# A decoder step on one core: the places of the depthwise convolution's VectorE steps

## The chip, the core and the metric

The kernel runs on one core of a Trainium2 chip. The metric is the device time of one execution in microseconds; less is better. A core has a matrix engine (PE, with its weight loads shown as PEld), a vector engine (DVE), a scalar engine (ACT), a general engine (POOL) and a sync engine (SP), which here does nothing but issue transfers from HBM. Each engine works through its own list of instructions in order, and waits for the others by semaphores.

## The reference

One layer of a decoder is computed for 512 prompt tokens and for 8 sequences of 4 new tokens each, 544 columns in all. Two branches read the same input projection: a convolution module and a stick-breaking attention. Cut to what matters here:

```
glu_a, glu_b, q, k, v, g_conv, g_att = split(x @ w_in)
u = glu_a * sigmoid(glu_b)                              # 512 channels
c = depthwise_conv(u, 31 taps) + conv_b                 # causal, per channel
conv_out = silu(layer_norm(c)) @ w_conv_proj
o = stick_breaking_attention(q, k, v)                   # samples: 4096 cached keys each
att_out = o @ w_att_proj
mixed = (sigmoid(g_conv) * conv_out + sigmoid(g_att) * att_out) @ w_out
x = layer_norm(alpha * x + mixed)
x = layer_norm(alpha * x + swiglu_ffn(x) + sigmoid(x @ w_ple_gate) * (p @ w_ple))
```

The cached keys and values of the samples lie in pages, 256 of keys and 256 of values, 256 KB each, which are found through a page table. They are 134 MB of the 222 MB that the kernel moves.

## The kernel before

Everything is held with the features on the 128 partitions and the tokens along the free axis. A dense product in near-full precision is made of three passes over a pair of parts, high and low, of both operands, so every weight tile is split by ACT (`wh`) and by DVE or POOL (`wl`) before PE uses it. Such a product writes a PSUM tile `g`; in the profile it reads `g<-xh,wh`, `g<-xl,wh`, `g<-xh,wl`. All products are recorded by `mm` (line 238), all transfers by `load` (line 228), and all DVE, ACT and POOL operations by one wrapper (line 146), so a reader goes by tile names rather than by lines.

The order of the instructions is written by a planner, the class `Weave`. It keeps one clock for PE (`wv.t`) and one for each other engine (`wv.dve`, `wv.act`, and `wv.dma` for transfers), and adds an assumed duration for each recorded operation. The work is a set of Python generators. The main one records the dense products; the side ones record the rest whenever the condition that they yielded last has come true on these clocks. So a condition decides where an instruction stands in its engine's list, and nothing of it is left at run time: on the chip an instruction waits for its operands and for its turn.

The generators that matter here:

- `main` makes the input projection in the order q, k, b, a, v for each of four groups of 128 channels, then the two sets of gates (tiles `ga`, `gc`), then the attention's projection (from the tiles `ohl`), then, after `yield done("conv")`, the convolution's projection (from `sh`, `sl`), then the output projection (tiles `m`), and from there the feed-forward part (`x1h`, `h`) and the embedding (`ph`).
- `prefetch` lets SP issue the pages, 32 groups of 8 key loads (`kv<-in_ck`) and 8 value loads (`kv<-in_cvv`) in turn. Every key load is preceded by the reading of a page number (line 657).
- `scores` and `decode` use them: group by group PE makes scores (`z<-kv`), ACT and DVE turn these into weights (`dz`, `dl`, `dp`), PE transposes them (`tp`) and multiplies with the values (`av<-kv`).
- `pa_pair` is the prompt's attention: scores into `z` and `tp`, weights `pa` with `pb` on ACT, DVE and POOL, sums into `o`. The values come by way of a transposition, which DVE copies out (`v<-tp`).
- `conv` is the depthwise convolution, all on DVE. For each of the four channel groups `i`, when its input `u` is there, it records 31 taps for the prompt's 512 columns (one `c<-u,cvt` and thirty `c<-u,cvt,c`), and two parts for the samples (`cs<-u`, `c<-cs`). Then follow the layer norm over all four groups (tiles `lnc`), the silu, and the split into `sh` and `sl`.

What paces `conv` before the change is one condition, tested after every second tap and before the sums of the samples' parts: `wv.dve < wv.t + CAHEAD`, that is, DVE's planned backlog is under 2.5 us (`CAHEAD`, line 1698). The generator has priority 3, behind those of the pages (0, 1) and of the attention (2).

Of the kernel before, what the change touches and what calls it, by code (L numbers as in the profile page):

```python
# [63 lines left out]
class Weave:  # L64
# [7 lines left out]
    def on(self, *aps):  # L72
        return At(max(self.ready.get(a.name, 0.0) for a in aps))
# [102 lines left out]
def step_kernel(ctx: ExitStack, tc: tile.TileContext, xT, pT, ck, cvv, state, pt, W, cv, cc, yT, kT, vT, cvo):  # L176
    nc = tc.nc
    wv = Weave()
# [10 lines left out]
    def done(f):  # L189
        return lambda: f in flag  # L190

    def spare(n):

        return lambda: cur["t"] <= 4 - n

    def drop():
        cur["t"] -= 1

    def slot(name, shape=(128, 2, NT), dt=F32):
        return big.tile(list(shape), dt, tag="s", bufs=NSLOT, name=name)  # L200

    def tmp(name):
        cur["t"] += 1
        return big.tile([128, NT], F32, tag="t", bufs=4, name=name)
# [42 lines left out]
    def calm():  # L247
        return max(wv.act, wv.dve) < wv.t + CALM

# [25 lines left out]
    def split(hi, lo, src, *then, eng=None):  # L275
        n = size(src)
        near = src.space != PSUM
        if near and end("dve", (n / 2 + 66) / 960, src) + VBIAS < end("act", (n + 112) / 1200, src):
            V.tensor_copy(out=hi, in_=src)
        else:  # L280
            S.activation(out=hi, in_=src, func=AF.Copy)

        def low():
            (tt if near and eng is None else V.tensor_tensor)(out=lo, in0=src, in1=hi.bitcast(F32), op=ALU.subtract)
            flag.update(then)
        if not then:
            low()
        else:
            wv.when(on(hi), low)

    def sigmoid(out, in_, t, t2, then, more=None):

        r = tmp("r")[:, :t.shape[1]]
        S.activation(out=t2, in_=in_, func=AF.Abs)
        r2 = halves(r) if len(in_.shape) == 3 else r
        n = size(in_)
        if end("dve", (n + 66) / 960, in_) + VBIAS < end("act", (n + 112) / 1200, in_):
            V.tensor_scalar(out=r2, in0=in_, scalar1=-1.0, scalar2=0.0, op0=ALU.mult, op1=ALU.max)
        else:
            S.activation(out=r2, in_=in_, func=AF.Relu, scale=-1.0)  # L300
        S.activation(out=t, in_=t, func=AF.Exp, scale=-1.0)
        S.activation(out=t, in_=t, func=AF.Ln, bias=1.0)

        def last():
            S.activation(out=out, in_=t, func=AF.Exp, scale=-1.0)
            flag.add(then)
            if more is not None:
                wv.when(on(out), more)

        def mid():  # L310
            tt(out=t, in0=r, in1=t, op=ALU.add)
            drop()
            wv.when(on(t), last)
        wv.when(on(t), mid)
# [551 lines left out]
    silu = []  # L866

    def conv():
        for g in range(2):
            c2 = slot("c")  # L870
            for e in range(2):
                i = 2 * g + e
                yield done(("u", i))
                u = us.pop(i)
                c = c2[:, e]
                a_ = c[:, 0:512]
                b_ = c[:, 512:544].rearrange("p (s q) -> p s q", q=4)
                us_ = u[:, 542:814].rearrange("p (s c) -> p s c", c=34)
                for k in range(KW):
                    w = cvt[:, CW + i * KW + k:CW + i * KW + k + 1]  # L880
                    a = u[:, k:k + 512]
                    if k == 0:
                        bb = cvt[:, CB + i:CB + i + 1]
                        V.tensor_scalar(out=a_, in0=a, scalar1=w, scalar2=bb, op0=ALU.mult, op1=ALU.add)
                    else:
                        V.scalar_tensor_tensor(out=a_, in0=a, scalar=w, in1=a_, op0=ALU.mult, op1=ALU.add)
                    if k % 2:
                        yield lambda: wv.dve < wv.t + CAHEAD
                for s in range(0, 8, 4):
                    yield spare(1)  # L890
                    t = tmp("cs")[:, :16 * KW].rearrange("p (s q k) -> p s q k", q=4, k=KW)
                    for q in range(4):
                        V.tensor_tensor(out=t[:, :, q], in0=us_[:, s:s + 4, q:q + KW],
                                        in1=cvt[:, CW + i * KW:CW + (i + 1) * KW].unsqueeze(1)
                                        .to_broadcast([128, 4, KW]), op=ALU.mult)
                    yield lambda: wv.dve < wv.t + CAHEAD
                    V.tensor_reduce(out=b_[:, s:s + 4], in_=t, op=ALU.add, axis=mybir.AxisListType.X)
                    del t
                    drop()
                V.tensor_scalar(out=b_, in0=b_, scalar1=cvt[:, CB + i:CB + i + 1], scalar2=None, op0=ALU.add)  # L900
                yield lambda: wv.dve < wv.t + CAHEAD
                del u, us_, a
                if i == 1:
                    tot = big.tile([128, NT], F32, tag="tot", bufs=1, name="tot")
                    V.tensor_tensor(out=tot, in0=c2[:, 0], in1=c2[:, 1], op=ALU.add)
                elif i > 1:
                    V.tensor_tensor(out=tot, in0=tot, in1=c, op=ALU.add)
            cp.append(c2)
        f = [slot("lnc") for i in range(3)]

        def each(g):
            x = cp[g]
            for e in range(2):
                i = 2 * g + e
                V.tensor_scalar(out=x[:, e], in0=x[:, e], scalar1=cvt[:, CG + i:CG + i + 1],
                                scalar2=cvt[:, CBB + i:CBB + i + 1], op0=ALU.mult, op1=ALU.add)
        yield from norm(cp, 2.0, NT, "o", f, tot, each, pace=calm)
        for g in range(2):
            yield on(cp[g])
            for e in range(2):  # L920
                t = f[g][:, e]
                yield calm
                yield spare(1)
                sigmoid(t, cp[g][:, e], t, t, ("silu", g, e))
                yield
        for g in range(2):
            x, t = cp[g], f[g]
            for e in range(2):
                yield done(("silu", g, e))
            yield on(t)  # L930
            yield calm
            V.tensor_tensor(out=x, in0=x, in1=t, op=ALU.mult)
            h, lo = slot("sh", dt=F32R), slot("sl", dt=F32R)
            yield on(x)
            split(h, lo, x, ("sl", g))
            silu.extend((h[:, e], lo[:, e]) for e in range(2))
        yield done(("sl", 0))
        yield done(("sl", 1))
        cp.clear()
        flag.add("conv")  # L940
# [146 lines left out]
    def residual():  # L1087
        x_hl.clear()
        for g in range(4):
            yield lambda: wv.dve < wv.t + CAHEAD  # L1090
            h, lo = (t.bitcast(F32) for t in x_tiles[g])
            r = slot("rr")
            V.tensor_tensor(out=r, in0=h, in1=lo, op=ALU.add)
            x_tiles[g] = h = lo = None
            yield lambda: wv.dve < wv.t + CAHEAD
            V.tensor_scalar(out=r, in0=r, scalar1=ALPHA, scalar2=None, op0=ALU.mult)
# [7 lines left out]
    def main():  # L1104
# [61 lines left out]
        vs = v2 = None  # L1166
        wv.add(prompt_attention(), 2)
        wv.add(conv(), 3)
        for w, m in ORDER:
            o = []  # L1170
# [525 lines left out]
GBIAS = 0.3  # L1696
DMA_AHEAD = 5.0
CAHEAD = 2.5
CALM = 1.5
WAHEAD = 5  # L1700
PSTEP = 1.0
# [106 lines left out]
```

## Time and profile before

| | |
|---|---|
| Median of 3 runs | 993.13 us (991.53 to 996.7) |
| The profiled execution's own time | 992.45 us |
| Its span | 990.6 us |
| Mean granted PE clock in it | 0.986 |
| PE busy | 950.3 us (96%) |
| DVE busy | 781.3 us (79%) |
| ACT busy | 539.2 us (54%) |
| POOL busy | 163.2 us (16%) |
| Moved by DMA | 222 MB, 224 GB/s over the span |
| The chain of waits that ended last | PE 74%, DVE 10%, DMA 9%, SP's queue 3% |

The span reaches from the first to the last instruction; the execution's own time is 1.85 us longer. A busy PE is not PE at its peak, since matmuls are pipelined and their ends are modelled. The kernel has two halves. Up to about 555 us pages stream in and everything shares the engines; from about 580 us on PE works through the feed-forward part almost without a pause. The convolution's taps lie between 43 and 266 us, its norm and silu between 267 and 373 us.

### The profile page before, as it was taken

How to read it: one execution, taken by the hardware profiler on the slowest of the kernel's cores; microseconds unless marked ns; L12 is line 12 of the kernel's file. 1: busy time of each engine (PE TensorE's matmuls, PEld its weight loads, DVE VectorE, ACT ScalarE, POOL GpSimd, SP SyncE). 2: the span in 40 equal slices, each digit the busy share in tenths (PEclk: the TensorE clock that was granted, in tenths of full speed). 3: DMA queues.
4: the chain of work that ended last, by engine and by line, in shares of the span. 5: the costliest groups of instructions: out<-in, count | busy, mean ns of one | idle time of the engine just before them, and what ended most of it. 6: DMA issues, size and time to landing. Idle time of an engine off the chain costs nothing.

```text
span 990.6 us, 22509 instructions
## 1 busy us (share of the span) xinstructions
PE 950.3 (96%) x8026; PEld 831.2 (84%) x8026; DVE 781.3 (79%) x1288; ACT 539.2 (54%) x1042; POOL 163.2 (16%) x147
## 2 busy tenths in 40 slices
PE   9989999999899999999999889999999999999995
PEld 7866566667677887788878789999999999999994
DVE  3798798999964666466698687999999999943366
ACT  4634766575786785244467564544554555622224
POOL 1230313223211102033343110000000000220020
PEclk9999899999999999999999899999999999999998
DMA  9948989999989999999999635223223221322302
GB/s 356 339 160 298 336 301 330 313 324 328 311 281 339 311 346 330 342 367 351 325 335 352 250 108 193 86 88 126 86 91 123 86 95 56 100 93 87 128 1 90
DMA packets 101393, 222.00 MB, mean 224 GB/s; under 512 B 11169, under 2 KB 14498, under 8 KB 101282
## 3 DMA queue, kind: packets, MB, share of 16 engines
q1 hardware_dynamic: 99410, 217.46, 62.5%
q10 hardware_dynamic: 1872, 3.11, 0.8%
q8 instruction: 63, 1.03, 0.4%
q14 instruction: 48, 0.39, 0.1%
HBM read 215.45 MB, written 5.07 MB: 223 GB/s over the span
## 4 chain that ended last, share of the span: by engine, by line
PE 74%; DVE 10%; DMA 9%; SPq 3%; issue 2%; ACT 2%; POOL 0%; ACTq 0%; DVEq 0%; POOLq 0%
PE g L238 44%; PE z L238 10%; PE av L238 9%; PE o L238 5%; PE tp L238 5%; DVE c L146 3%; DMA kv<-in_cvv 2%; SPq L228 2%; DMA kv<-in_ck 2%; DVE pb L146 2%; DMA wr<-in_W 2%; PE tp L243 1%; DMA xr<-in_xT 1%; SPq L657 1%; DMA wa<-in_W 1%
## 5 line engine op out<-in xcount | busy, mean ns | idle before, releaser
L146 ACT ACTIVATE wh<-wr 128x512 fp32r<-128x512 f32 x236 | 146.9, 628 | 201.1 <-PE g L238 99.8
L146 DVE TENSOR_TENSOR wl<-wr,wh 128x512 fp32r<-128x512 f32 x196 | 135.1, 694 | 52.1 <-ACT wh L146 50.8
L146 POOL TENSOR_TENSOR wl<-wr,wh 128x512 fp32r<-128x512 f32 x44 | 70.2, 1598 | 493.0 <-DVE pw L146 259.8
L238 PE MATMUL g<-xh,wh 128*128 128x272 f32 (+1 forms) x512 | 127.6, 320 | 0.3 <-ACT wh L146 0.3
L238 PE MATMUL g<-h,wh 128*128 128x272 f32 x704 | 122.2, 290 | 0.0
L238 PE MATMUL g<-xl,wh 128*128 128x272 f32 (+1 forms) x512 | 119.3, 304 | 0.8 <-DVE xl L146 0.8
L238 PE MATMUL g<-xh,wl 128*128 128x272 f32 (+1 forms) x512 | 118.8, 303 | 0.2 <-POOL wl L146 0.2
L146 DVE SCALAR_TENSOR_TENSOR c<-u,cvt,c 128x512 f32<-128x512 f32 x120 | 111.6, 930 | 3.3
L238 PEld LDWEIGHTS g<-h,wh 128*128 128x128 f32 x704 | 103.2, 189 | 0.3
L238 PEld LDWEIGHTS g<-xh,wh 128*128 128x128 f32 x512 | 82.9, 191 | 22.2 <-issue 17.5
L238 PEld LDWEIGHTS g<-xl,wh 128*128 128x128 f32 x512 | 83.7, 191 | 3.6 <-DVE xl L146 1.5
L238 PEld LDWEIGHTS g<-xh,wl 128*128 128x128 f32 x512 | 83.1, 191 | 4.0 <-POOL wl L146 0.9
L238 PE MATMUL g<-h,wl 128*128 128x272 f32 x352 | 80.1, 289 | 0.0
L146 ACT ACTIVATE wh<-wq 128x512 fp32r<-128x512 f32 x87 | 54.5, 628 | 40.5 <-PE g L238 29.5
L238 PE MATMUL z<-kv,qblk 128*32 128x256 f32 x1024 | 64.6, 381 | 1.1 <-DMA kv<-in_ck 1.1
L238 PE MATMUL g<-x1h,wh 128*128 128x272 f32 (+2 forms) x216 | 64.0, 296 | 0.0
L238 PE MATMUL av<-kv,dp 128*32 128x512 f32 x512 | 63.8, 612 | 0.0
L146 DVE TENSOR_TENSOR wl<-wq,wh 128x512 fp32r<-128x512 f32 x75 | 54.6, 733 | 11.4 <-ACT wh L146 11.0
L238 PE MATMUL g<-x1l,wh 128*128 128x272 f32 (+2 forms) x216 | 62.6, 290 | 0.0
L238 PE MATMUL g<-x1h,wl 128*128 128x272 f32 (+2 forms) x216 | 62.6, 290 | 0.0
L146 ACT ACTIVATE pa<-pa 128x384 f32<-128x384 f32 (+1 forms) x96 | 52.5, 555 | 17.2 <-DVE pa L146 15.6
L238 PEld LDWEIGHTS g<-h,wl 128*128 128x128 f32 x352 | 58.0, 188 | 0.0
(315 smaller groups left out, 2352.8 us busy)
## 6 DMA issues: line engine op xcount, KB each, us to landing
kv<-in_ck SPq DMA_DIRECT2D x256, 256.0 KB, 4.4
kv<-in_cvv SPq DMA_DIRECT2D x256, 256.0 KB, 5.4
wr<-in_W SPq DMA_DIRECT2D x98, 512.0 KB, 4.2
wq<-in_W SPq DMA_DIRECT2D x37, 512.0 KB, 5.1
wa<-in_W SPq DMA_DIRECT2D x12, 512.0 KB, 10.2
xr<-in_xT SPq DMA_DIRECT2D x8, 272.0 KB, 5.6
out_yT<-pw SPq DMA_DIRECT2D x6, 272.0 KB, 2.3
out_kT<-qk ACTq DMA_DIRECT2D x4, 272.0 KB, 6.1
```

What stands on the lines that cost most here:

```text
L146: fn(**kw)
L228: eng.dma_start(out=out, in_=in_)
L238: T.matmul(out, lhsT=lhsT, rhs=rhs, start=start, stop=stop)
L243: T.transpose(out, in_, ident)
L657: reg[col] = nc.sync.value_load(ptt[0:1, col:col + 1], min_val=0, max_val=POOL - 1)
```

## The change

The pace of `conv` is set otherwise. A counter runs through the steps of the convolution: 31 taps and 2 sample parts for each channel group, 132 steps in all. After step n the generator now yields until the planner's PE clock has reached `CONV_T0 + n * CONV_DT`, that is 20 + 1.9 n us, and DVE's planned backlog is under `CAHEAD` as before. The condition now stands after every tap, where it stood after every second one. The last step may so be recorded from 270.8 us of the planner's clock on. No operation is added, removed or resized.

```
     def conv():
+        step = [0]
+
+        def even():
+
+            step[0] += 1
+            t = CONV_T0 + step[0] * CONV_DT
+            return lambda: t <= wv.t and wv.dve < wv.t + CAHEAD
         for g in range(2):
...
                         V.scalar_tensor_tensor(out=a_, in0=a, scalar=w, in1=a_, op0=ALU.mult, op1=ALU.add)
-                    if k % 2:
-                        yield lambda: wv.dve < wv.t + CAHEAD
+                    yield even()
                 for s in range(0, 8, 4):
...
-                    yield lambda: wv.dve < wv.t + CAHEAD
+                    yield even()
                     V.tensor_reduce(out=b_[:, s:s + 4], in_=t, op=ALU.add, axis=mybir.AxisListType.X)
...
 CAHEAD = 2.5
+CONV_T0 = 20.0
+CONV_DT = 1.9
```

Since the planner decides by its clocks, other generators' instructions move too. Three places are shown, as the engines' lists have them before and now.

DVE, the start of the second channel group (`u` is its input, `c` its sums, `dp`, `dl`, `dz` the weights of a group of pages, `pb` and `pa` the prompt's attention). Before:

```order
L146 TENSOR_SCALAR c<-u,cvt 128x512
L146 SCALAR_TENSOR_TENSOR c<-u,cvt,c 128x512 x9
L146 TENSOR_TENSOR wl<-wq,wh 128x512
L146 TENSOR_SCALAR dp<-dz 128x256
L146 SCALAR_TENSOR_TENSOR dl<-dl,cnew,dp 128x256
L146 TENSOR_TENSOR dz<-dz,dl 128x256
```

Now:

```order
L146 TENSOR_SCALAR c<-u,cvt 128x512
L146 SCALAR_TENSOR_TENSOR c<-u,cvt,c 128x512 x2
L146 CAST wh<-wq 128x512
L146 SCALAR_TENSOR_TENSOR c<-u,cvt,c 128x512
L146 TENSOR_SCALAR pb<-pa 128x512
L146 SCALAR_TENSOR_TENSOR pb<-pb,pa 128x512
L146 TENSOR_TENSOR pa<-pa,pb 128x512
L146 TENSOR_SCALAR dp<-dz 128x256
```

A run of ten taps ahead of the next weights has become one of three and a single one.

PE, the first scores of a group of pages (`z<-kv`; `tp<-cct,anew` is a transposition, the `g` products belong to the input projection). Before:

```order
L243 MATMUL tp<-cct,anew 128x128
L238 MATMUL g<-xh,wh 128x512
L238 MATMUL g<-xl,wh 128x512
L238 MATMUL g<-xh,wl 128x512
L238 MATMUL g<-xh,wh 128x272 x2
L238 MATMUL g<-xl,wh 128x272 x2
L238 MATMUL g<-xh,wl 128x272 x2
L238 MATMUL z<-kv,qblk 32x256 x16
```

Now:

```order
L243 MATMUL tp<-cct,anew 128x128
L238 MATMUL g<-xh,wh 128x512
L238 MATMUL g<-xl,wh 128x512
L238 MATMUL g<-xh,wl 128x512
L238 MATMUL g<-xh,wh 128x512
L238 MATMUL g<-xl,wh 128x512
L238 MATMUL g<-xh,wl 128x512
L238 MATMUL z<-kv,qblk 32x256 x16
```

Six products of 272 columns that stood ahead of the first scores now stand behind them; the three of 512 columns stood ahead of the transposition before.

PE, the last scores of a group of pages (the `ph` products are the embedding's, the `x1h` ones the feed-forward part's). Before:

```order
L238 MATMUL g<-ph,wh 128x272 x2
L238 MATMUL g<-pl,wh 128x272 x2
L238 MATMUL g<-ph,wl 128x272 x2
L238 MATMUL z<-kv,qblk 32x256 x16
L238 MATMUL o<-ln,on_m 128x256
```

Now:

```order
L238 MATMUL g<-x1h,wh 128x256
L238 MATMUL g<-x1l,wh 128x256
L238 MATMUL g<-x1h,wl 128x256
L238 MATMUL z<-kv,qblk 32x256 x16
L238 MATMUL g<-x1h,wh 128x256
L238 MATMUL g<-x1l,wh 128x256
L238 MATMUL g<-x1h,wl 128x256
```

The last scores have moved ahead, past products that now follow them: counted from the program's start, 2292 products `g` stood ahead of the last scores, and 2247 do now.

## The prediction

> **What bounds the kernel now.** I read the table by stretches first: it tells which stage of the 990.6 us could move at all. Its columns are the stretch, then busy time of each engine, the granted PE clock, the DMA share and GB/s.
>
> ```profile
> core 0: us, PE busy (x) PEld busy (x) DVE busy (x) ACT busy (x) POOL busy (x), PEclk, DMA share, GB/s
> 50.00:275.00 225.00, 206.94 (x1752) 152.82 (x1751) 205.76 (x329) 135.90 (x282) 57.70 (x55) 0.97 0.87 301
> 275.00:400.00 125.00, 124.15 (x1093) 98.36 (x1091) 81.32 (x122) 92.85 (x179) 19.79 (x18) 1.00 0.93 323
> 400.00:545.00 145.00, 143.94 (x1256) 116.14 (x1259) 101.32 (x164) 74.52 (x155) 44.55 (x38) 1.00 0.97 345
> 600.00:990.60 390.60, 378.72 (x2989) 377.50 (x2988) 321.43 (x528) 175.18 (x304) 21.92 (x11) 0.99 0.27 95
> ```
>
> DVE is 91% busy from 50 to 275 us and 65% in the next stretch; the DMA engines are at 87%, 93% and 97%. After 600 us only PE matters. The same stretches for the tile `c` alone show what the convolution takes of DVE:
>
> ```profile
> 50.00:275.00 225.00, 117.19 (x133) 0.97 0.87 301
> 275.00:400.00 125.00, 14.32 (x12) 1.00 0.93 323
> ```
>
> It is 57% of DVE's work in the stretch where DVE is full. Next the waits of PE between 45 and 275 us (who waited for what: us, times, longest):
>
> ```profile
> PE tp L243 <- DVE v L146: 7.8, 4, 4.4
> PE tp L243 <- ACT pa L146: 6.3, 3, 2.2
> PE z L238 <- ACT dz L146: 2.2, 1, 2.2
> PE tp L238 <- ACT dp L146: 0.8, 1, 0.8
> PE o L238 <- DVE tot L146: 0.7, 1, 0.7
> ```
>
> These 17.8 us are pauses of PE behind DVE, directly or by way of ACT. If PE alone set the end, they would be the prize. But the pages also have to arrive. SP's own queue shows what that takes:
>
> ```profile
> 332.15 8.67 SPq L228 DMA_DIRECT2D kv<-in_ck  x8
> ...
> 342.61 0.36 SPq L228 DMA_DIRECT2D wr<-in_W  x1
> 343.16 3.07 SPq L228 DMA_DIRECT2D kv<-in_cvv  x5
> 347.08 0.34 SPq L228 DMA_DIRECT2D kv<-in_ck  x1
> ```
>
> One group of pages keeps SP issuing from 332.15 to 347.08, without a pause worth the name: 8.67 us for eight key loads, 3.07 for five value loads. So the stream of pages has a pace of its own, some 15 us a group, that no DVE work enters unless SP itself waits. And PE is tied to it. Two rows show the scores of a group halted until its keys land; between 290 and 425 us such halts are all that is left of PE's waits for pages:
>
> ```profile
> 299.46 1.89 PE L238 MATMUL z<-kv,qblk 128*32 128x256 f32 x26 [0.26 <-DMA kv<-in_ck]
> 389.52 1.89 PE L238 MATMUL z<-kv,qblk 128*32 128x256 f32 x26 [0.59 <-DMA kv<-in_ck]
> PE z L238 <- DMA kv<-in_ck: 0.8, 2, 0.6
> ```
>
> I conclude that before the feed-forward half two things end together, PE's list and the stream. A pause of PE that is removed before 299 us is mostly given back as a halt there, unless the stream comes earlier too. The first half's end is so a matter of SP's waits.
>
> **The change, part by part.** Nothing is added: the same DVE instructions stand elsewhere. The convolution's taps last 0.75 us as a median, and the mean is higher because some take over 1.5. By the order, tap 31 stands behind 306 products `g` (294 before), tap 62 behind 570 (450), tap 93 behind 780 (672) and tap 124 behind 1065 (900). Before, the last tap stood behind 14 groups of scores; tap 106 stands there now. So 18 of 124 taps leave the full stretch. At the mean of the group, 117.19 us over 133, they are 16 us of 205.76: DVE falls from 91% to 84% there, and rises from 65% to 78% after it. The relief is modest.
>
> The first term is the longest wait of SP, between 62 and 100 us, with PE's and DVE's lists around it:
>
> ```profile
> SPq L228 <- PE z L238: 13.6, 2, 13.4
> 43.78 4.81 DVE L146 SCALAR_TENSOR_TENSOR c<-u,cvt,c 128x512 f32<-128x512 f32 x5
> 49.10 3.53 DVE L146 SCALAR_TENSOR_TENSOR c<-u,cvt,c 128x512 f32<-128x512 f32 x2
> 57.36 0.68 DVE L146 COPY v<-tp 128x512 f32<-128x512 f32 x1
> 64.22 0.41 PE L238 MATMUL g<-xh,wh 128*128 128x272 f32 x2
> 65.06 1.93 PE L238 MATMUL z<-kv,qblk 128*32 128x256 f32 x32
> ```
>
> SP stands still for 13.4 us because all page buffers are full and the first scores have not read them; these stand in PE's list behind a transposition whose bank DVE's `v` copy frees at 58 us, and that copy stands behind eight taps. The order now has eight taps there again: the grid of 20 + 1.9 n has already run past the first steps when `u` comes, so it holds nothing back. That wait therefore stays but for the six products of 272 columns that left their place ahead of the scores: from 64.22 to 65.06, **0.8 us**.
>
> The second term is SP's other waits between 80 and 350 us:
>
> ```profile
> SPq L228 <- DVE wl L146: 4.5, 2, 2.4
> SPq L228 <- DMA out_vT<-vt: 3.5, 1, 3.5
> SPq L228 <- DMA out_kT<-qk: 1.9, 1, 1.9
> SPq L228 <- POOL wl L146: 1.8, 2, 1.2
> ```
>
> The splits on DVE and POOL are 6.3 us, and a less crowded DVE can make them end earlier; the two at DVE lie in the stretch that now gets the last taps, though. Bounds: nothing, or, with the stores that ACT issues late, all 11.7. I take a third of the splits, **2.1 us**, nearer to nothing because of where they lie.
>
> The third term is bytes and issues: ahead of the last page 59 weight loads stand in SP's order where 60 stood. By the rows of SP's queue one costs 0.55 us of its time (342.61 to 343.16); by the 345 GB/s of the stretch its 512 KB cost 1.5. I take **1.0 us**. The stream so ends 3.9 us earlier.
>
> Against this, the price on the other side. The rows around the last scores:
>
> ```profile
> 523.75 1.48 SPq L228 DMA_DIRECT2D kv<-in_ck  x2
> 532.70 1.93 PE L238 MATMUL z<-kv,qblk 128*32 128x256 f32 x32
> 536.59 0.28 PE L238 MATMUL g<-x1h,wh 128*128 128x256 f32 x1
> 536.71 0.28 PE L238 MATMUL g<-x1l,wh 128*128 128x256 f32 x1
> kv<-in_ck SPq DMA_DIRECT2D x256, 256.0 KB, 4.4
> ```
>
> The last key load is issued at 524.9 (the second of the two from 523.75) and, at the median of 4.4 us, lands at 529.3; the scores start at 532.70, 3.4 us after it. Now 45 products fewer stand ahead of them, at 0.12 us each (536.59 to 536.71) **5.4 us**, which PE has to do afterwards. PE could come to the last scores at 532.7 - 5.4 = 527.3, less what it gains in pauses. The stream allows 529.3 - 3.9 + 0.3 (a halt as at 299 us) = 525.7. Half of the 13.4 us of pauses behind the first `v` copy would bring PE there, so I take the stream. Behind the last scores stood 990.6 - 532.7 = 457.9 us; now there are 5.4 more. The sum is 525.7 + 457.9 + 5.4 = 989.0 us of span, 1.6 less than before. With the 1.85 us around the span and the 0.7 us by which the median lies above the profiled execution this is **991.5 us**.
>
> The Trainium skill speaks against the second and third term: its page "DMA: Bandwidth & Descriptors", section "Issuing engines are not separate DMA queues", says that the time which the sequencer takes to initiate a transfer is usually small beside the transfer. By it SP's waits would be hidden under the queue and the weight load would cost its bytes; the sum would be 0.8 + 1.5 = 2.3 us of stream and a median of 993.1. The rows of SP's queue, solid for 15 us a group, disagree, so I keep the terms.
>
> What the moved work is hidden behind: the 16 us of taps that go past 275 us lie in a stretch with 43 us of idle DVE (125 less 81.32). What is late next is the silu. Its cover is read from these rows:
>
> ```profile
> L238 PE MATMUL g<-sh,wh x64: 282/288/394, 419.4 to 449.3; 128*128 128x272 f32 x64
> L146 DVE TENSOR_TENSOR sl<-c,sh x2: 1278/1832/2387, 367.9 to 370.9; 128x1088 fp32r<-128x1088 f32 x2
> 386.81 0.63 PE L238 MATMUL g<-ohl,wh 128*128 128x512 f32 x2
> ...
> 387.51 0.63 PE L238 MATMUL g<-ohl,wh 128*128 128x512 f32 x2
> ```
>
> Before, the split ended at 373.3 and its reader started at 419.4, 46 us later. In the order now 44 products from `ohl` (three from 386.81 to 387.51, 0.23 each, 10 us) and one group's scores and values (under 4) stand between: 14 us.
>
> **The rivals.** *Faster, because both bounds give way.* The pauses vanish and every SP wait listed above goes with them: the stream gains 0.8 + 11.7 + 1.0 = 13.5, the span is 990.6 - 3.4 + 0.3 + 5.4 - 13.5 = 979.4, the median 982; with two thirds of the waits, 986. For it speak the pauses, and the clock that falls behind one of them, where PE's share of a stretch of 10 us, the granted clock and the DMA share read:
>
> ```profile
> 100.00:110.00 10.00, 9.17 (x48) 0.70 1.00 344
> ```
>
> Against it: only 7 points of DVE's load go, and two of the four SP terms are stores or lie late. In a sentence of its own: "Perfetto Trace Analysis", section "Optimization Strategy", in the Trainium skill would have it so, since it tells to relieve the engines that PE idles for.
>
> *Slower, because the silu comes too late.* The convolution's projection waits in PE's list, and everything behind it, the pages' scores too. It decides once the norm and silu run over 14 us later than their place in the order. They took from 267 to 373 us; now the chain has to fit between about 315 and 407, while DVE is at 78% and not 65%. A lateness of 22 us would cost 8: 999. Against it: DVE has not lagged by more than the 4.4 us of the longest `v` pause.
>
> *Nothing moves in time.* The grid is on the planner's clock; if the chip is always behind it, the backlog condition alone decides and the list differs by chance. Then only the six products and the unit come off the stream, 1.8 us, and PE halts for it: 529.3 - 1.8 + 0.3 + 457.9 + 5.4 = 991.1 of span, a median of 993.6.
>
> **How the numbers follow.** Forecast 0.55, its own range 986 to 995: 986 with 5.5 us more of SP's waits gone, 995 with nothing of the stream gained. Faster rival 0.27, silu 0.12, nothing moves 0.06. A measurement of this kernel tells about 0.5% from no change, 5 us. Faster by more: nine tenths of the rival and 0.15 of the forecast, 0.33. Slower by more: most of the silu's 0.12 and a little of the rest, 0.13. Within: 0.54. For 8 in 10 the range reaches to the full price of the faster rival, 982, and on the other side nearly to the silu's and to the 998.5 of a stream that gains nothing while the last scores still start 3.4 us behind their keys: 998.
>
> **What would show it.** Right: SP's wait for `z` stays near 13 us; PE's waits for `v` and `pa` shrink, yet PE halts more for `in_ck` between 290 and 540 us; the last key load is issued some 4 us earlier; DVE at 84% up to 275 us. Wrong: the 13.4 us wait gone (then the faster rival), a wait of PE for `sl` at `g<-sh` (the silu), or a stream whose last key load comes later than at 524.9.

## The result and the profile after

The changed kernel takes **1007.73 us** (median of 4 runs, 1004.59 to 1013.15) against 992.8 for the kernel before beside it: 1.0154 times as long, 95% interval 1.0124 to 1.0183. It is slower, by 1.5%. The profiled execution is the slowest of the four, 1013.15 us with a span of 1011.4, so its rows show some 5 us more than the median has.

The table by stretches of the changed kernel, with the columns of the one shown of before:

```profile
core 0: us, PE busy (x) PEld busy (x) DVE busy (x) ACT busy (x) POOL busy (x), PEclk, DMA share, GB/s
50.00:275.00 225.00, 208.63 (x1765) 149.88 (x1764) 194.90 (x318) 136.11 (x282) 55.45 (x54) 0.98 0.88 296
275.00:400.00 125.00, 120.38 (x1061) 96.69 (x1059) 80.93 (x126) 86.73 (x170) 17.22 (x13) 1.00 0.94 324
545.00:600.00 55.00, 41.83 (x454) 37.05 (x453) 43.91 (x82) 26.81 (x62) 17.09 (x16) 0.94 0.48 184
```

DVE has fallen to 87% of the first stretch (91% before). But PE now idles 4.6 us between 275 and 400 us (0.9 before), and 13 of the 55 us from 545 on. To compare at equal work I cut both executions at two points of PE's list: the first product of the attention's projection (`g<-ohl`, 22 groups of scores ahead of it in both) and the first of the feed-forward's pairs (`z<-x1h`). Before, and then after:

```profile
45.00:385.20 340.20, 321.85 (x2777) 246.22 (x2776) 278.36 (x442) 225.25 (x454) 72.82 (x64) 0.98 0.89 308
385.20:609.30 224.10, 216.62 (x1925) 180.77 (x1924) 164.52 (x281) 119.62 (x248) 59.11 (x54) 0.98 0.84 300
609.30:990.60 381.30, 369.42 (x2920) 368.20 (x2918) 314.19 (x516) 170.55 (x295) 21.92 (x11) 0.99 0.26 90
```

```profile
45.00:387.90 342.90, 324.06 (x2777) 244.94 (x2777) 270.01 (x441) 220.68 (x448) 68.78 (x62) 0.99 0.90 306
387.90:630.00 242.10, 221.47 (x1922) 182.59 (x1921) 174.21 (x287) 120.95 (x247) 60.22 (x58) 0.97 0.78 277
630.00:1011.40 381.40, 369.44 (x2920) 368.23 (x2918) 314.64 (x516) 170.44 (x295) 21.72 (x11) 0.99 0.26 89
```

The last stretch is the same to 0.1 us. The first, where the change was made, is 2.7 us longer, but that is no more than the spread between executions: a_hold and a_pace below, whose lists are the same up to that point by their traces, reach it at 384.8 and 385.5 us. The middle one is **18.0 us longer**: PE idles 20.6 us of it instead of 7.5, and the same work takes it 4.9 us more, at a granted clock of 0.97 instead of 0.98. So the loss lies behind the convolution's taps, in a stretch where the change moved nothing on purpose.

Of PE's waits for DVE between 385 and 640 us, those that grow most, before:

```profile
PE g L238 <- DVE sg L146: 2.5, 1, 2.5
PE g L238 <- DVE pw L146: 0.7, 1, 0.7
```

and after:

```profile
PE g L238 <- DVE sg L146: 7.6, 3, 4.1
PE g L238 <- DVE ga L146: 4.8, 1, 4.8
PE g L238 <- DVE pw L146: 2.1, 1, 2.1
```

Two places carry 9.9 of the 13.1 us by which the pauses grow. The first is the drain of a gate's product into `ga`, whose bank PE needs for the attention's projection. DVE and PE around it:

```profile
397.30 1.69 DVE L146 TENSOR_SCALAR rr<-rr 128x1088 f32<-128x1088 f32 x1
398.91 1.29 DVE L146 TENSOR_TENSOR rr<-xh,xl 128x1088 f32<-128x1088 f32 x1
400.23 1.67 DVE L146 TENSOR_SCALAR rr<-rr 128x1088 f32<-128x1088 f32 x1
401.82 0.68 DVE L146 TENSOR_TENSOR ga<-g,ga 128x512 f32<-128x512 f32 x1
402.56 1.22 PE L238 MATMUL g<-ohl,wh 128*128 128x512 f32 x2 [4.80 <-DVE ga L146]
```

The residual's operations (`rr`, recorded by `residual`) stand ahead of the drain and PE halts 4.8 us. Before, the convolution's norm was long over there; now its tail (`lnc`, up to 394 us) and the residual share DVE just ahead of `ga`. Before, the first drain began 9.0 us after the first `g<-ohl` (385.18):

```profile
394.18 0.68 DVE L146 TENSOR_TENSOR ga<-g,ga 128x512 f32<-128x512 f32 x1
```

Now it begins 13.9 us after it (387.93). Three of the four scalings of the residual take 1.67 to 1.77 us each, where all four took at most 0.73 before: some 3 us of the delay. The second place is the embedding (`g<-ph`), whose bank waits for the feed-forward's `sg`:

```profile
592.19 6.59 DVE L146 TENSOR_TENSOR tl<-tw,th 128x544 fp32r<-128x544 f32 x6
598.71 0.68 DVE L146 TENSOR_TENSOR wl<-wr,wh 128x512 fp32r<-128x512 f32 x1
599.31 0.41 DVE L146 TENSOR_TENSOR sg<-g,sg 128x256 f32<-128x256 f32 x1
599.77 0.52 PE L238 MATMUL g<-ph,wh 128*128 128x272 f32 x2 [4.09 <-DVE sg L146]
```

Six splits of the token sums (`tl`) stand in a row ahead of it. Before, the last such `sg` stood ahead of the row of splits:

```profile
577.63 0.42 DVE L146 TENSOR_TENSOR sg<-g,sg 128x256 f32<-128x256 f32 x1
580.45 4.99 DVE L146 TENSOR_TENSOR tl<-tw,th 128x544 fp32r<-128x544 f32 x6
```

### The profile page after: what moved, and what is told of

Same layout as the page of the kernel before. It is cut to its first block, busy times and chain, and to the rows that moved or that the text cites. A ratio compares the mean times of both kernels' runs of the same rounds, so it can differ in the third digit from the quotient of the medians.

```text
span 1011.4 us, 22525 instructions
## 1 busy us (share of the span) xinstructions
PE 956.8 (95%) x8026; PEld 831.7 (82%) x8026; DVE 783.4 (77%) x1293; ACT 535.7 (53%) x1035; POOL 160.1 (16%) x149
## 4 chain that ended last, share of the span: by engine, by line
PE 75%; DVE 9%; DMA 8%; issue 3%; SPq 3%; ACT 2%; POOL 0%; ACTq 0%; DVEq 0%; POOLq 0%
PE g L238 44%; PE z L238 11%; PE av L238 9%; PE o L238 5%; PE tp L238 4%; DMA kv<-in_ck 4%; DMA kv<-in_cvv 2%; DVE c L146 2%; PE tp L243 2%; SPq L228 2%; DVE pb L146 1%; SPq L657 1%; DMA wr<-in_W 1%; DVE rr L146 1%; DVE tl L146 1%
## 5 line engine op out<-in xcount | busy, mean ns | idle before, releaser
L146 DVE SCALAR_TENSOR_TENSOR c<-u,cvt,c 128x512 f32<-128x512 f32 x120 | 104.5, 871 | 2.6
L238 PEld LDWEIGHTS g<-xh,wh 128*128 128x128 f32 x512 | 82.3, 190 | 22.4 <-issue 18.2
L238 PE MATMUL z<-kv,qblk 128*32 128x256 f32 x1024 | 70.3, 386 | 8.5 <-DMA kv<-in_ck 8.4
L238 PEld LDWEIGHTS z<-kv,qblk 128*32 128x32 f32 x1024 | 34.5, 110 | 37.0 <-issue 12.4
```

The costliest lines, as they stand in the source:

```text
L146: fn(**kw)
L238: T.matmul(out, lhsT=lhsT, rhs=rhs, start=start, stop=stop)
```

## The experiments

All times of kernels are medians, beside the kernel before at 992.8 to 993.5 us, and the ranges behind them are 95% intervals of the ratio to it. "Products ahead" are PE's instructions into `g` ahead of an instruction in the planned order; the last scores have 2292 ahead of them before and 2247 in the change. In the table, the start of `g<-ohl` and the stretch behind it come from one profiled execution of each kernel, cut at the points used above; differences of some 3 us there say little, since after and a_hold differ by 3.1 us at `g<-ohl` with the same list up to it.

| kernel | products ahead of the last scores | start of `g<-ohl`, us | from there to the pairs, us | median, us | ratio to before |
|---|---|---|---|---|---|
| before | 2292 | 385.2 | 224.1 | 992.8 | |
| after | 2247 | 387.9 | 242.1 | 1007.7 | 1.0154 |
| e1_fine | 2223 | 395.4 | 231.5 | 1008.9 | 1.0166 |
| e2_front | 2247 | 391.9 | 239.4 | 1014.8 | 1.0226 |
| e6_pairs | 2250 | 392.5 | 231.1 | 1003.7 | 1.0102 |
| e7_dt23 | 2139 | 388.4 | 237.8 | 1009.4 | 1.0166 |
| e5_resid | 2217 | 387.1 | 232.3 | 998.8 | 1.0056 |
| a_pace | 2247 | 385.5 | 236.0 | 1004.5 | 1.0116 |
| a_hold | 2292 | 384.8 | 231.2 | 999.3 | 1.0073 |
| a_margin2 | 2310 | 375.1 | 235.5 | 995.4 | 1.0022 |
| a_margin2_pace | 2310 | 378.6 | 235.9 | 996.8 | 1.0038 |
| a_mix30 | 2307 | 378.1 | 232.2 | 993.6 | 1.0006 |
| a_mix31 | 2298 | 376.3 | 236.5 | 995.4 | 1.0032 |
| resid_margin3 | 2292 | 382.7 | 234.9 | 996.9 | 1.0036 |
| resid_hold | 2292 | 383.0 | 240.3 | 1007.0 | 1.0153 |
| b_margin15 | 2223 | 393.3 | 228.8 | 1005.3 | 1.0114 |
| b_margin2 | 2298 | 385.0 | 228.4 | 998.6 | 1.0058 |
| b_resid | 2280 | 384.1 | 232.2 | 1000.2 | 1.0074 |
| b_early2 | 2268 | 386.0 | 229.6 | 996.5 | 1.0043 |
| b_hold | 2310 | 386.9 | 228.5 | 999.7 | 1.0071 |

(b_margin15 has one group of scores more ahead of `g<-ohl` than the others, so its two columns are shifted by that group.)

**First round: which part of the change, which wait.** e1_fine keeps only the finer question, after each tap, without the grid:

```
-            return lambda: t <= wv.t and wv.dve < wv.t + CAHEAD
+            return lambda: wv.dve < wv.t + CAHEAD
```

> The backlog condition after every tap, as in the change, but no grid (the grid's time is left out of the condition). In the order the last tap stands behind 936 products g (900 before, 1065 in the change) and the last instruction of the norm behind 1483, ahead of the first product from ohl at 1537. Late-tail theory (the change loses because the norm and silu now share DVE with the attention projection's ga products and the residual): the pause of 4.8 us at g<-ohl is gone, and the time is 993 to 998. Rival (what costs is the finer test, which lets the scores and everything behind them move ahead in PE's list; here the last scores stand behind 2223 products, 2247 in the change, 2292 before): 1003 to 1010, as the change.

1008.9 us (1.0134 to 1.0199): as slow as the whole change although its taps lie early. Its wait behind `ga` is gone, as foreseen, and yet the loss is there, most of it ahead of the attention's projection, which starts 10.2 us later than before. The theory that the taps come too late falls as the sole cause. e2_front spreads the first two channel groups only:

```
-            t = CONV_T0 + step[0] * CONV_DT
+            t = CONV_T0 + step[0] * CONV_DT if step[0] <= 66 else 0.0
```

> The change with the grid for the first two channel groups alone; the steps of the last two are recorded as early as they fit, tested after every tap. The last tap stands behind 980 products, the norm ends behind 1536, just at the first product from ohl. Late-tail theory: the pause at g<-ohl is at most half of its 4.8 us, 996 to 1002. Rival (the list of PE, last scores behind 2247 products as in the change): 1003 to 1010.

1014.8 us (1.0203 to 1.0249), over both ranges, and PE still waits 5.2 us behind `ga`. Why this kernel is the slowest of all no run shows. e7_dt23 makes the grid wider:

```
-CONV_DT = 1.9
+CONV_DT = 2.3
```

> The change with 2.3 us a step in place of 1.9. The last tap stands behind 1375 products, and the split of the silu behind 1642, after the first product g<-sh in PE's list at 1633. Late-tail theory: PE now waits for the silu itself, a pause of several us at g<-sh: 1012 to 1030. Rival (the list, last scores behind 2139 products): slower too, but by products left over behind the pages and without a pause at g<-sh: 1008 to 1016.

1009.4 us (1.0146 to 1.0187), in the second range, and even here the profile shows no halt of PE for `sl` at `g<-sh`. e5_resid takes what stands ahead of `ga` away:

```
     def residual():
         x_hl.clear()
+        yield done("ga")
```

> The change, with the residual's eight DVE operations (rr) recorded only after the attention projection's last ga product. Late-tail theory: the four pairs of rr no longer stand ahead of the first ga product, so the pause of 4.8 us and the slow clock behind it (1.7 us of the 25 us from 400 to 425) go: 1000 to 1003. Rival: nothing but the place changes, the last scores move further ahead (2217): 1005 to 1012.

998.8 us (1.0038 to 1.0074), faster than either range: 9 us of the 15 are back. Its wait behind `ga` between 385 and 640 us:

```profile
PE g L238 <- DVE ga L146: 1.0, 1, 1.0
```

So that pause, 4.8 us in the trace, is in all likelihood a real part of the loss; the rest of the 9 us goes with other places that moved with it, and no run parts the two.

**Second round: the list or the taps.** The planner's margin ahead of a group of scores (`KMARGIN`) has nothing to do with the convolution, and turning it moves the scores in the list. b_margin15 is the kernel before, its taps early, with

```
-KMARGIN = 1.0
+KMARGIN = 1.5
```

> The kernel before (taps as early as they fit), with the planner's margin ahead of a group of scores raised from 1.0 to 1.5 us. The taps stay early (tap 124 behind 886 products, 900 before), but the planner's list comes out with the last scores behind 2223 products instead of 2292, which is where the changed kernels have them (2223 to 2247). Theory of the list (what costs is the place of the last scores and the products and splits that are left behind them): slower by as much as the change, 1003 to 1012 us, with the pairs starting at 620 us or later (609 before, 630 after the change). Theory of the late taps (what costs is DVE work behind 275 us): the same as before, 990 to 997 us.

1005.3 us (1.0082 to 1.0147): a kernel without any of the change, as slow as with it. a_margin2 is the changed kernel, its taps late, with `KMARGIN = 2.0`:

> The changed kernel with that margin at 2.0 us. The taps stay late (tap 124 behind 1079 products), and the last scores stand behind 2310 products (2247 in the change, 2292 before). Theory of the list: most of the loss is back, 993 to 1000 us, the upper end since the residual still stands ahead of the drain of ga. Theory of the late taps: 1005 to 1010 us, as the change.

995.4 us (1.0008 to 1.0036). Late taps, and nearly the time of before. That is inside the range of the list theory. These two together take the loss away from the taps and give it to the list that the planner makes around them. a_pace changes one number in the token sums' condition of the changed kernel:

```
-            return wv.dve < wv.t + 0.7
+            return wv.dve < wv.t + 0.2
```

> The changed kernel, and only the token sums' splits are held to a DVE backlog of 0.2 us in place of 0.7. The list is the change's up to there; the longest row of splits in a row on DVE falls from six pairs of instructions to four. If the pauses of PE behind sg between 580 and 605 us (8.4 us in the change, 3.2 before) are a real part of the loss, 1001 to 1005 us; if they only take time that another wait would take, 1006 to 1010 us.

1004.5 us (1.0077 to 1.0155), in the first range and 3.2 us below the change, but the two intervals overlap, so the price of the splits ahead of `sg` is not shown. What is shown is that PE's wait for `sg` between 385 and 640 us, 7.6 us in the change, has mostly gone:

```profile
PE g L238 <- DVE sg L146: 1.9, 2, 1.3
```

resid_margin3 is e5_resid with `KMARGIN = 3.0`:

> The changed kernel with the residual held back until ga is drained (which alone gave 998.8 us) and with the margin at 3.0 us, which puts the last scores behind 2292 products, as before the change. Theory of the list: nothing of the loss is left, 988 to 995 us. Theory of the late taps: as with the residual alone, 997 to 1002 us.

996.9 us (1.0014 to 1.0058), a miss for the list theory, whose range ended at 995: repairs do not simply add up.

**Third round: controls.** b_margin2 is the kernel before with `KMARGIN = 2.0`, b_resid the kernel before with the edit of e5_resid.

> The kernel before with the margin ahead of the scores at 2.0 us in place of 1.5: the control of b_margin15 (1005.3 us). The same knob is turned, by more, but here the list comes out with the last scores behind 2298 products (2292 before, 2223 at 1.5). Theory of the list: the time of before, 990 to 996 us. If the larger margin itself costs, as every group of scores stands later: 1003 us or more.

> The kernel before with the residual held back until ga is drained: the control of that edit, which took the changed kernel from 1007.7 to 998.8 us. Before has no pause behind ga, and its last scores move from 2292 to 2280 products. If the edit's gain was the pause behind ga, there is nothing to gain here: 991 to 997 us. If a later residual is good by itself: 985 to 988 us.

998.6 us (1.0037 to 1.008) and 1000.2 us (1.0045 to 1.0102): the first lies between its two ranges, the second above both. In b_resid the later residual is in the way elsewhere (PE waits 1.6 us for `rr` at 497 us). The place of the last scores is not all, and an edit that repairs one list harms another. e6_pairs has the grid without the finer question:

```
-                    yield even()
+                    step[0] += k % 2 == 0
+                    if k % 2:
+                        yield even()
```

> The other half of the change alone: the grid of 20 + 1.9 n, but the question is put after every second tap, as before, and not after each. The taps are spread as in the change (tap 124 behind 1080 products) and the last scores stand behind 2250. Theory of the list: as slow as the change, 1003 to 1010 us, although the finer question (alone 1008.9) is gone. If the two parts each had a cost of their own: 999 us or less.

1003.7 us (1.0074 to 1.0131), inside the range of the list theory: the grid alone costs some 10 us and the finer question alone some 15, where both together cost 15. They are not two costs that add up. a_margin2_pace joins two repairs:

> The changed kernel with both repairs that helped: the margin at 2.0 us (995.4 us alone) and the token sums held to a backlog of 0.2 us (1004.5 alone, 3 us under the change). If the two add up, 991 to 994 us, level with before; if the pauses behind sg are gone in the kernel with the margin already (its pauses between 570 and 585 us sum to 4.9 us, 3.2 before), 994 to 997 us. Under 988 us, which would beat before, is not expected: the last key load was issued at 522.9 us there against 524.9 before, so at most some 2 us of the stream are to be had.

996.8 us (1.0019 to 1.0056), at the upper end: nothing is added.

**Fourth round: the last group of scores alone.** a_hold and resid_hold hold the last group in the changed kernel and in e5_resid until 2292 products stand ahead of it; b_hold does so in the kernel before with 2310; b_early2 cuts the margin of the last two groups in the kernel before.

```
+        cur["g"] = cur.get("g", 0) + (out.name[0] == "g")
...
             yield KMARGIN
+            yield lambda: c < 31 or cur.get("g", 0) >= 2292
```

```
-            yield KMARGIN
+            yield KMARGIN if c < 30 else 0.3
```

> The changed kernel, and only the last group of scores is held until 2292 products stand ahead of it (2247 in the change); up to the group before it the list is the change's, word for word, and so are the late taps and the pause behind ga. If the place of the last scores is itself what costs, PE meets them 5.4 us later but leaves that much less behind them and has scores again to do while DVE drains the embedding: the pauses between 530 and 640 us fall from 13 us towards the 6 of before, 998 to 1003 us. If the place only goes along with a list that is bad all over, nothing changes: 1006 to 1010 us.

> The same hold in the changed kernel with the later residual (998.8 us, last scores behind 2217 products, 8 us of pauses in the tail). If the place costs: 992 to 996 us. If not: 997 to 1001 us.

> The kernel before, and only the last two groups of scores have their margin cut from 1.0 to 0.3 us, which puts the last ones behind 2268 products in place of 2292; all ahead of them, the taps too, is as before. If the place costs, 24 products too early are worth 3 us of work left behind and some of the pauses: 996 to 1001 us. If it does not: 991 to 995 us.

> The kernel before with the last group held until 2310 products stand ahead of it, 18 more than it has. If later is better without end, 988 to 991 us; if the place of before is where pages and PE's list meet, PE's list is done waiting for nothing and the decoding of the last group comes later by 2.2 us: 993 to 997 us.

a_hold 999.3 us (1.0048 to 1.0099): 8 us gained by moving one group, the list ahead of it being the same. b_early2 996.5 us (1.0016 to 1.0071), as forecast for a place that costs. With the smaller margin PE comes to the last group but one ahead of its keys; before, such halts between 385 and 640 us summed to 0.6 us, here to:

```profile
PE z L238 <- DMA kv<-in_ck: 2.9, 2, 2.6
```

b_hold 999.7 us (1.0047 to 1.0095): worse than forecast, so later is no better than earlier. Its waits between 385 and 640 us show what takes over:

```profile
PE tp L244 <- ACT dz L146: 3.8, 1, 3.8
PE av L238 <- ACT dp L146: 2.3, 1, 2.3
```

With the last group so late, nothing covers the chain from its scores to its weights. resid_hold 1007.0 us (1.012 to 1.0186) refutes its forecast: at the same place as in a_hold PE waits 8.5 us for `sg` again.

```profile
PE g L238 <- DVE sg L146: 8.5, 4, 4.1
```

So the place of the last scores matters, but, as the waits suggest, by what stands beside it on DVE and ACT. No count of products foretells the time.

**Fifth round: where the relief goes.** The same margin of 2.0 us, cut at the same two points, first with the early taps (b_margin2), then with the late ones (a_margin2):

```profile
45.00:385.00 340.00, 321.80 (x2775) 245.22 (x2774) 280.46 (x438) 223.47 (x451) 81.30 (x71) 0.99 0.91 307
385.00:613.40 228.40, 215.51 (x1924) 179.30 (x1923) 162.98 (x287) 120.80 (x248) 51.70 (x48) 0.99 0.84 296
```

```profile
45.00:375.10 330.10, 318.16 (x2774) 242.77 (x2774) 270.27 (x450) 221.05 (x447) 62.86 (x58) 0.99 0.92 318
375.10:610.70 235.60, 219.46 (x1925) 180.42 (x1924) 170.82 (x296) 120.16 (x244) 56.98 (x48) 0.98 0.81 286
```

Here the kernel with the spread taps does what the change was made for: PE comes to the attention's projection (the expectations below call it the out-projection) 9.9 us earlier, with 11.9 us of pauses instead of 18.2. Whether the spreading does it or the list that came with it, these two do not part: at a margin of 1.0 PE came no earlier (387.9 against 385.2). Behind it 7.2 us are given back. Even so the change is no loss at this margin, 998.6 us without it and 995.4 with it (1.0037 to 1.008 against 1.0008 to 1.0036), and with the later residual it makes no difference that is clear of the noise, 1000.2 and 998.8 us. The same edit costs 15 us in one list, nothing in a second and saves some 3 in a third. PE's longest pause behind the projection is 5.5 us with the late taps (3.8 at the same place in b_margin2). ACT's and PE's rows of a_margin2:

```profile
541.70 0.63 ACT L146 ACTIVATE x1h<-rr 128x512 fp32r<-128x512 f32 x1
542.23 0.40 ACT L146 ACTIVATE dz<-dz 128x256 f32<-128x256 f32 x1
542.68 0.69 PE L243 MATMUL tp<-cct,dz 128*128 128x128 f32 x2 [5.50 <-ACT dz L146]
```

ACT works without a gap on the layer norm's drains (`rr`, `x1h`) from 533.7 us on, and the last group's `dz` stands behind them. a_mix30 and a_mix31 try other orders there, the margin at 2.0 but for the last two groups (1.0) or the last one (0.3, with the pace of a_pace):

```
-            yield KMARGIN
+            yield 2.0 if c < 30 else 1.0
```

> The changed kernel with the margin at 2.0 us for all groups of scores but the last two, which keep 1.0. With 2.0 for all (995.4 us) PE came to the out-projection's first half 10 us earlier than before and gave it all back behind it, 5.5 us of it in one pause ahead of the last group's transpositions. Here that group stands 3 products earlier and the splits stand apart (at most three in a row). If the gain ahead of the out-projection is real and only given back by the order behind it, 986 to 993 us, and the stretch up to the out-projection stays at 330 us. If it is given back whatever stands there, since pages and the last group's chain come no earlier, 994 to 999 us.

> The same with the last group's margin alone cut, to 0.3 us, which puts the last scores behind 2298 products (2310 with 2.0 for all, 2292 before), and the token sums held to a backlog of 0.2 us. The same two readings: 986 to 993 us if the order behind the out-projection is what gives the gain back, 994 to 999 us if the gain is lost whatever stands there.

a_mix30 993.6 us (0.9996 to 1.0016) lies between the two ranges, level with before; its halt behind `dz` is still there, 5.7 us. a_mix31 995.4 us (1.0019 to 1.0044) lies in the second. The gain ahead of the projection stayed in both (378.1 and 376.3 us), and both gave it back. No kernel here beats the one before.

## Why the prediction was wrong, point by point

Two terms of the sum failed. It was 525.7 us up to the last scores and 463.3 behind them; the profiled execution has 538.1 and 473.3. That execution is 5.4 us over the median, so the 22.4 us between the two spans compare with the 16.2 us between forecast and median.

- **"The first half's end is so a matter of SP's waits": wrong as a bound for this kernel.** The forecast put the last scores at 525.7 us by the stream. They start at 538.1, and no halt for keys stands ahead of them; the last keys had landed at 537.1. PE is late by itself. From the first `g<-ohl` to the last scores it took, before and then after:

```profile
385.20:532.70 147.50, 145.98 (x1233) 115.60 (x1231) 105.83 (x166) 74.88 (x153) 46.34 (x44) 1.00 0.96 339
387.90:538.10 150.20, 142.77 (x1189) 109.81 (x1189) 106.12 (x165) 71.34 (x143) 39.28 (x40) 0.99 0.94 325
```

  That is 2.7 us more with 45 products fewer. PE idles 7.4 us instead of 1.5, and 4.8 of them are the wait for `ga`, for which the sum had no term. The stream is late as well. Before, from 400 us on:

```profile
400.00:440.00 40.00, 40.00 (x308) 31.09 (x311) 19.81 (x34) 13.02 (x26) 6.09 (x7) 1.00 0.98 347
440.00:480.00 40.00, 40.00 (x377) 33.90 (x370) 28.08 (x44) 18.09 (x36) 14.72 (x14) 1.00 0.97 349
480.00:520.00 40.00, 39.29 (x368) 31.18 (x367) 31.85 (x52) 24.82 (x53) 15.53 (x13) 1.00 0.95 332
```

and after, where the pause for `ga` lies in the first row:

```profile
400.00:440.00 40.00, 37.45 (x258) 26.54 (x259) 25.20 (x40) 13.74 (x26) 4.24 (x9) 0.96 0.92 318
440.00:480.00 40.00, 38.80 (x359) 32.04 (x358) 25.86 (x44) 18.14 (x36) 6.40 (x8) 1.00 0.96 334
480.00:520.00 40.00, 39.97 (x373) 31.84 (x373) 28.35 (x50) 18.80 (x39) 12.66 (x12) 1.00 0.91 310
```

  Missing are 29 + 15 + 22 GB/s over 40 us each, at 345 GB/s 7.7 us of stream. The last key load is issued at 533.0, 8.1 us later than before and not 3.9 earlier. By the prediction's own test ("a stream whose last key load comes later than at 524.9") this step is wrong. From 362 us to that load SP's own waits sum to 15.8 us where they were 10.3, those for DVE's `wl` to 3.6 where they were 1.1: part of the lateness comes through SP after all, the other way than forecast. And 2 to 3 us of it are this execution's own, since a_hold and a_pace, with the same list up to there, issue that load at 529.7 and 530.9. In a_margin2 it was issued at 522.9, 2 us earlier than before. The earliest of all runs was 521.5, near the 521.0 of the forecast, in resid_hold, and that kernel took 1007.0 us: an earlier stream did not decide the end.
- **The first two terms of the stream gave nothing.** SP's wait for `z` stayed, as told: 13.1 us, where 13.4 less 0.8 was forecast. The four waits of the second term fell from 11.7 to 6.5 us between 80 and 350 us, but SP's waits for PE rose there (for `av` from 1.3 to 3.2 us, for `z` from 0.4 to 2.4). The sum had the stream 2.9 us ahead by then. The first key load of the 22nd group, before and after, shows it level:

```profile
362.71 1.45 SPq L228 DMA_DIRECT2D kv<-in_ck  x2
362.83 1.45 SPq L228 DMA_DIRECT2D kv<-in_ck  x2
```

  The third term, one weight load less, can't be read apart from the 8.1 us.
- **The pauses before 275 us moved as told.** PE's waits between 45 and 275 us after the change:

```profile
PE tp L243 <- DVE v L146: 6.8, 3, 4.4
PE z L238 <- DMA kv<-in_ck: 6.2, 7, 1.8
```

  The waits for `v` fell by 1.0 us, those for `pa` from 6.3 to 0.3, and halts for keys rose from 0.2 to 6.2: taken away and given back, step for step what "is mostly given back as a halt" said. DVE is at 87% up to 275 us, not at 84.
- **The second step that failed is the price of the list, "45 products fewer ... 5.4 us, which PE has to do afterwards".** It counted PE's time for the products and nothing of the DVE and ACT work between them. Behind the last scores now lie 1011.4 - 538.1 = 473.3 us, against 463.3 in the sum: 10.0 us more, 7.3 of it pauses, mostly behind `sg` and `pw`, and the rest a slower PE. a_hold, which puts the last group back, is 8.4 us faster, not 5.4. But the same hold makes e5_resid 8.3 us slower (998.8 to 1007.0), so this is the price of a place in one list, and no price of 45 products.
- **"What is late next is the silu" named the wrong reader.** The norm's tail did run late on DVE, and the split ended at 414.0 instead of 373.3, but PE reads it from 429.5 on and never waits for `sl`. The one who suffered was `ga`, which the working never looked at. A pause of 4.8 us there, and a time of 998.8 us with 1.0 us of it left: this term was missing. The rival that gave 999 us had the right sign and the wrong place.
- **The faster rival's first half exists**: 9.9 us ahead of the attention's projection with another margin. Its second half, that the gain reaches the end, no run shows.

What stays open: why the stretch behind the projection takes 224.1 us in the kernel before and 228 or more in each of the nineteen others, changed or not. Single collisions were shown (`ga`, `sg`, `dz`); that their sum is what sets before apart was not shown for each kernel. Nor was it tested whether the planner's constants simply suit the list of before, so that almost any other list meets some collision; the two margins tried on the kernel before fit that, and do not prove it.

## What to carry to other kernels

Where a planner with assumed clocks writes the order, a small edit reshuffles every engine's list, and the reshuffling can cost more than the edit moves: compare the whole lists, and ask of each bank that PE needs what now stands ahead of its drain. Before a loss is put down to the edit, turn an unrelated knob of the planner: here that alone cost 0.6 and 1.1%. Try the edit under that other setting too: at a margin of 2.0 us the change that cost 15 us saved 3. And a price of "so many products left behind" has to hold the drains of those products on DVE and ACT, not PE's time alone.

## What the runs showed of the hardware

**A DVE operation between two tiles in SBUF often takes twice as long while POOL works.** The taps, all of one shape, as the pages before and after have them (count, then busy and mean ns):

```profile
L146 DVE SCALAR_TENSOR_TENSOR c<-u,cvt,c 128x512 f32<-128x512 f32 x120 | 111.6, 930 | 3.3
...
L146 DVE SCALAR_TENSOR_TENSOR c<-u,cvt,c 128x512 f32<-128x512 f32 x120 | 104.5, 871 | 2.6
```

Worked out from the rows of before: 75 taps with no POOL work beside them have a median of 0.75 us, 36 that lie for over half of their time beside POOL work 1.65. The residual's scaling after the change shows the same, 0.73 us alone and 1.77, 1.69 and 1.67 beside POOL's splits. After the change 26 taps lie so, not 36; that gave DVE 7 us, which the prediction did not count. The row of six splits ahead of `sg` took 6.59 us where six of 0.71 would be 4.3. The Trainium skill's page "SBUF — State Buffer", section "SBUF: two separate sides", has it that a DVE operation with two inputs in SBUF, as a tap is, and a POOL operation that reads SBUF shut each other out of a shared pair of ports, and whichever starts first holds it for the whole instruction. The slow taps agree with it. Not all rows do: the splits `wl`, with two inputs as well, have a median of 0.69 us beside POOL work against 0.68, and in the kernel before the residual's scaling at 392.31 us took 0.73 beside POOL's copies.

**A long pause of PE is paid for twice.** Behind the 4.1 us pause that ends at 599.77 the granted clock of the next 10 us is 0.83:

```profile
600.00:610.00 10.00, 10.00 (x66) 10.00 (x66) 4.58 (x8) 5.61 (x10) 1.66 (x1) 0.83 0.28 105
```

and 0.83 too from 402 to 412 us, behind the pause for `ga`: some 1.7 us of PE's speed each, on top of the pause. Shorter pauses do it only sometimes. In the kernel before, 2.2 us with another 0.8 just behind them gave the 0.70 shown from 100 us on, but 2.5 us ahead of 578.1 gave nothing:

```profile
578.00:588.00 10.00, 9.18 (x69) 8.96 (x70) 10.00 (x16) 7.66 (x14) 2.69 (x2) 1.00 0.18 59
```

What decides between the two the runs here do not show.
